# The product of w_out and the gate, split half by half in two units and fetched in the last

## The chip, the cores and the metric

The kernel runs on one core of one Trainium2 chip. The metric is the time of one execution on the device in microseconds (us), as the median of several runs. Beside that there is one execution recorded by the profiler, whose instructions, semaphores and transfers the text reads. The engines are called PE (TensorE; PEld is its weight load), DVE (VectorE), ACT (ScalarE), POOL (GpSimd) and SP (SyncE, which issues nearly all DMAs here).

## The reference

One decoder layer in float32, sequence of 2048 rows, width 1024, one sequence, followed by a final RMSNorm:

```python
mod = silu(c) @ w_ada + b_ada
shift, scale, gate = split(mod, 3)
h = rmsnorm(x, g_norm) * (1 + scale) + shift
proj = h @ w_in                       # gq gk gv ga gz sq sk sv sz
o_gla = rmsnorm(gla_chunked(gq, gk, gv, log_a)) * silu(gz)
o_swa = sliding_window_sink_attention(rope(sq), rope(sk), sv) * silu(sz)
y = concat([o_gla, o_swa]) @ w_out
x = x + gate * y
return rmsnorm(x, g_final)
```

The gate multiplies each of the 1024 output columns, so it can be taken into w_out: `y * gate` is the mixed rows times the matrix `w_out * gate`. The kernel does this. Each float32 matrix product is made of three products of float32r parts: a high part (the rounded value) and a low part (the remainder); high by high, high by low, low by high.

## The kernel before

**Units.** The sequence is cut in four units of 512 rows (NU = 4, u = 0 to 3). For each unit the kernel projects the normalised rows with w_in, in eleven slots of columns named sz0, kv, sq0, qk0, gv0, gz0, sq1, sz1, qk1, gv1, gz1 (the order of ORDER; the first unit begins with three of them side by side and has its own order). A slot takes 96 or 48 matmuls and is read out by ACT, DVE and POOL. When its inputs are there, the unit's attention tiles (`swa_tile`, four for each of two key heads) and its linear attention (`gla`, one for each of two pairs of heads; the first after gv0, the second after gv1) are emitted behind the slot. `norm(u + 1)`, which makes the next unit's rows `hh` and `hl`, is emitted behind gv0. The mixed rows go to DRAM (`mixd`). After the last unit come 16 output tiles (`out_tile`), each 48 matmuls with the output weights `wo`, the final RMSNorm and a store; they are bound by PE.

**The weights of the projection** are split into parts once, in the first unit, and kept in DRAM as `wc`; the later units fetch both parts (2 times 512 KB twice for each slot) one slot ahead.

**The output weights.** `late_rows` (line 561) is emitted once, behind slot sz0 of the last unit (line 1335). It works on two halves of 512 columns, i = 0 and 1. For a half it makes the gate row: eight loads `wg` of 256 KB, eight multiply-adds on DVE into `acc` (named gate), a split into two parts `ga`, two matmuls with ones into the PSUM tile `pg`, the load of the bias `bg`, and one addition. Then for each of eight tiles of w_out (k = 0 to 7) it loads `raw` (named wor), multiplies it with the gate on DVE, copies the high part on ACT and makes the low part on DVE. For k = 0 to 3 (WO_EARLY) the two parts (woh, wol) go into the `hp` buffers that the unit before has left and stay on the chip. For k = 4 to 7 (WO_LATE) they (wox, woy) are stored to DRAM as `woc`, and `last_rows` (line 599) fetches them at the end, when the last unit's own `hh` and `hl` are no longer needed.

**Buffers.** A tag is a ring of buffers, handed out in program order: a tile waits until the one that had its buffer before is no longer read. What matters here:

- `xs`, two buffers: in `norm` the eight `xn`, one `dgl`, the eight `xt`; in `late_rows` the `wg`, `ga` and `bg`; later residuals of the output.
- `r1`, one buffer: `rstd1` of `norm`, and `acc`.
- `st`, three buffers: in the first unit the raw weights; in `late_rows` `raw`, and for k = 4 to 7 also both parts; later residuals of the output.
- `px`, one PSUM buffer: `pr` of `norm`, `pg`, and in `gla` first `pu`, then one of the two `po`.

**The order of issue** is written out ahead of time. Every instruction is recorded with its engine, an estimated duration and its dependences (class `Order`); `issue` (line 210) then plays the program through in estimated time. Whenever an engine is free it takes, of the instructions that are ready, the one with the lowest key. The key is the place in the program plus a lift: -600 (LIFT) for what is urgent, +400 (LATER) for what can wait. A DMA is reckoned as its bytes over 370 GB/s behind what is already under way, and 1.8 us (lines 303 and 304). The order found is fixed for each engine, so on the chip an instruction whose input is late holds all that stand behind it on that engine.

Of the kernel before, what the change touches and what calls it, by code (L numbers as in the profile page):

```python
# [8 lines left out]
F32 = mybir.dt.float32  # L9
F32R = mybir.dt.float32r  # L10
I32 = mybir.dt.int32
AF = mybir.ActivationFunctionType
ALU = mybir.AluOpType
# [4 lines left out]
P = 128  # L18
D = 1024
S = 2048  # L20
KT = D // P
NB = 512
NU = S // NB
# [30 lines left out]
NORM_AT = 'gv0'  # L54
ORDER0 = ['gv0', 'qk1', 'kv', 'sq0', 'sz1', 'sq1', 'gv1', 'gz1']
ORDER = ['sz0', 'kv', 'sq0', 'qk0', 'gv0', 'gz0', 'sq1', 'sz1', 'qk1', 'gv1', 'gz1']
LATE_AT = 'sz0'
WO_EARLY, WO_LATE = (0, 1, 2, 3), (4, 5, 6, 7)
WARM0, WARM = 14, 13
WITH_V = (1, 3, 5, 7)  # L60
# [2 lines left out]
LATER = 400  # L63
# [267 lines left out]
def free_size(ap):  # L331
    n = 1
    for d in list(ap.shape)[1:]:
        n *= d
    return n
# [48 lines left out]
def layer_kernel(ctx, tc, x, xT, w_ada, w_gate, b_cols, b_gate, g_cols, c_cols, pos, inv_freq,  # L384
                 w_in, w_dec, g_head, sinks, w_out, g_fin, out):
    nc = tc.nc
    od = Order(tc)
    V, A, G, SY = [Engine(od, e) for e in ("V", "A", "G", "SP")]
# [12 lines left out]
    hp = Pool("hp", HB)  # L401
    wp = Pool("wp", 2)
    stp = Pool("stp", STB)
    mm = Pool("mm", 2, PSUM)
    att = Pool("att", 1, PSUM)
# [4 lines left out]
    def f(ap):  # L410
        return ap.bitcast(F32)


    def mmul(o, l, r, start, stop, bank=None):
        n, m, k = free_size(r), free_size(l), l.shape[0]
        mode = cell = None
        if l.dtype == F32:
            dur = 2 * max(0.107, n / 1200)
            if k <= 64:
                mode, cell = "rows", l.start_partition()  # L420
            elif m <= 64:
                mode, cell = "cols", o.start_partition()
        else:
            dur = max(0.112, n * 1.05 / 2400 + 0.006)
        return od.add("PE", lambda: T.matmul(o, l, r, start=start, stop=stop), dur,  # L425
                      [l, r] + ([] if start else [o]), [bank if start and bank is not None else o],
                      mode=mode, cell=cell)
# [25 lines left out]
    ones_r = const.tile([P, P], F32R, name="ones_r")  # L453
# [61 lines left out]
    s_c = const.tile([P, KT], F32, name="s_c")  # L515
# [42 lines left out]

    gfin = []

    def late_rows():

        for i in range(2):
            sl = slice(i * NB, (i + 1) * NB)
            acc = keep.tile([P, NB], F32, name=f"gate{i}", tag="r1")
            for k in range(KT):
                wg = stp.tile([P, NB], F32, name=f"wg{i}{k}", tag="xs", bufs=2)
                SY.dma_start(wg, w_gate[:, k, sl])
                if k == 0:
                    V.tensor_scalar(acc, wg, s_c[:, 0:1], None, op0=ALU.mult)  # L570
                else:
                    V.scalar_tensor_tensor(acc, wg, s_c[:, k:k + 1], acc,
                                           op0=ALU.mult, op1=ALU.add)
            parts = [stp.tile([P, NB], F32R, name=f"ga{i}{j}", tag="xs", bufs=2) for j in range(2)]
            A.copy(parts[0], acc)
            V.tensor_tensor(parts[1], acc, f(parts[0]), ALU.subtract)
            pg = att.tile([P, NB], F32, name=f"pg{i}", tag="px")
            for j in range(2):
                mmul(pg, ones_r, parts[j], j == 0, j == 1)
            bg = stp.tile([P, NB], F32, name=f"bg{i}", tag="xs", bufs=2)  # L580
            SY.dma_start(bg, b_gate[:, sl].broadcast_to([P, NB]))
            V.tensor_tensor(acc, pg, bg, ALU.add)
            for k in range(KT):
                raw = stp.tile([P, NB], F32, name=f"wor{k}{i}", tag="st")
                SY.dma_start(raw, w_out[k * P:(k + 1) * P, sl])
                V.tensor_tensor(raw, raw, acc, ALU.mult)
                if k in WO_EARLY:
                    h_ = hp.tile([P, NB], F32R, name=f"woh{k}{i}", tag="hh")
                    l_ = hp.tile([P, NB], F32R, name=f"wol{k}{i}", tag="hl")
                else:  # L590
                    h_, l_ = [stp.tile([P, NB], F32R, name=f"wo{j}{k}{i}", tag="st") for j in "xy"]
                wo[k, i] = h_, l_
                A.copy(h_, raw)
                V.tensor_tensor(l_, raw, f(h_), ALU.subtract)
                if k not in WO_EARLY:
                    for j in range(2):
                        SY.dma_start(f(woc[:, j, k, sl]), f(wo[k, i][j]))

    def last_rows():

        for k in WO_LATE:
            for i in range(2):
                wo[k, i] = [hp.tile([P, NB], F32R, name=f"wo{j}{k}{i}", tag=f"h{j}") for j in "hl"]
                for j in range(2):
                    SY.dma_start(f(wo[k, i][j]), f(woc[:, j, k, i * NB:(i + 1) * NB]))
        for i in range(2):
            gfin.append(near.tile([P, NB], F32, name=f"gf{i}", tag=f"qk{i}", bufs=2))
            SY.dma_start(gfin[i], g_fin[:, i * NB:(i + 1) * NB].broadcast_to([P, NB]))
# [3 lines left out]
    woc = dram.tile([P, 2, KT, D], F32R, name="woc")  # L612
    wo = {}
# [82 lines left out]
    hh = [None] * KT  # L696
    hl = [None] * KT
# [163 lines left out]
    def proj_n(w, n, sink):  # L861

        c = NB // n
        for t in range(TPU):
            ts = slice(t * P, (t + 1) * P)
            if t % c == 0:
                p = mm.tile([P, c, NB // c], F32, name=f"pn{t}", tag="mm")
            for k in range(KT):
                mm3(p[:, t % c, :n], hh[k][:, ts], hl[k][:, ts], w[0][k], w[1][k],
                    k == 0 and t % c == 0, k == KT - 1 and t % c == c - 1, p)  # L870
            if t % c == c - 1:
                urgent(sink, t - c + 1, p)
# [160 lines left out]
    def sink_kv(u):  # L1033
        def sink(t, ps):
            tt = u * TPU + t
            kt = keep.tile([P, 2, 2, 64], F32, name="kr", tag="kr", bufs=2)
            v = keep.tile([P, 2, 2, 2, 64], F32R, name="vs", tag="v", bufs=VB)
            rope(kt, ps[:, :, 0:128].rearrange("p t (h d) -> p t h d", h=2), 2, tt)
            pv = ps[:, :, 128:256].rearrange("p t (h d) -> p t h d", h=2)
            A.copy(v[:, :, :, 0], pv)  # L1040
            V.tensor_tensor(v[:, :, :, 1], pv, f(v[:, :, :, 0]), ALU.subtract)
            for i in range(2):
                vs[tt + i] = v[:, i]
            for i in range(2):
                kr[tt + i] = kt[:, i]
        return sink
# [183 lines left out]
    def loader(i, lift=LIFT):  # L1230

        if i < len(todo):
            od.lift = -lift
            w = load_w(todo[i][0], todo[i][1])
            loaded[i] = w
            if todo[i][0] == 0:
                for k in range(0, KT, 2):
                    w[2](k)
                od.lift = LATER
                w[3]()  # L1240
            else:
                for k in range(0, KT, 4):
                    w[4](k, k + 4)
            od.lift = 0
# [29 lines left out]
    keep = Pool("keep", 1)  # L1274
# [11 lines left out]
    ga = keep.tile([P, TPU, 32], F32, name="ga")  # L1286
# [15 lines left out]
    for i, (u, name) in enumerate(todo):  # L1302
        kind, g = name[:2], int(name[2:] or 0)
        if u > 0 and name == ORDER[0]:
            hh, hl = nexth[u]
        loader(i + 1, LIFT if i else 0)
        w = loaded.pop(i)
        if kind == "kv":
            proj_n(w, 256, sink_kv(u))
        elif kind == "sq":  # L1310
            qrs[u, g] = {}
            proj_n(w, 256, sink_sq(u, g, qrs[u, g]))
        elif kind == "gv":
            proj_n(w, SLOT_N[name], sink_gv(g))
        else:
            proj_t(w, sinks_of[kind](g))
        seen.add((u, name))
        if kind == "kv":
            k_rows(u)
        for what, g, need in (("S", 0, ("kv", "sz0", "sq0")), ("S", 1, ("kv", "sz1", "sq1")),  # L1320
                              ("G", 0, ("qk0", "gv0")), ("G", 1, ("qk1", "gv1")),
                              ("Z", 0, ("qk0", "gz0", "gv0")), ("Z", 1, ("qk1", "gz1", "gv1"))):
            if name in need and all((u, n) in seen for n in need):
                if what == "S":
                    for t in range(TPU):
                        swa_tile(u, g, t, qrs[u, g])
                elif what == "G":
                    rts[u, g] = gla(u, g)
                else:
                    gla_gate(u, g, rts[u, g])  # L1330
        if u < NU - 1 and name == (NORM_AT if u else NORM_AT0):
            od.lift = -LIFT
            norm(u + 1)
            od.lift = 0
        if u == NU - 1 and name == LATE_AT:
            late_rows()
    last_rows()
    for t in range(S // P):
        out_tile(t)
# [54 lines left out]
```

## Time and profile before

| What | us |
|---|---|
| Time, median of three runs | 862.0 |
| Time, lowest and highest | 861.47, 865.98 |
| Profiled execution, its own time | 860.93 |
| Its span, first to last instruction | 859.2 |
| Second unit, first sz0 matmul to the third unit's | 170.3 to 337.4 |
| Third unit | 337.4 to 498.7 |
| Last unit, to the first output matmul | 498.7 to 667.3 |
| Output tiles on PE | 667.4 to 852.4 |

The profile's page gives for each engine its busy time, its share of the span and its count of instructions. Nearly all instructions are issued through two helpers, so in the rows L378 stands for everything on ACT, DVE, POOL and SP, L425 for matmuls and L430 for transposes; the reader goes by the names of tiles, written out<-in. A row of a tile has the count, the shortest, median and longest duration in ns, the first and last start in us, and the shape. A row of the waits says who waited for whom, for how long in total, how often, and the longest. In a timeline the bracket at the end of a row holds the engine's idle time before it and what ended that. Rows of transfers have the size and the median time from issue to landing. Matmuls are pipelined and their ends are modelled, so short stalls of PE are hidden in its busy time.

### The profile page before, as it was taken

Reading aid. Unit: us, or ns where it says so; the run is one execution under the profiler, and the core shown is the slowest. Engines: PE = TensorE matmul, PEld = TensorE weight load, DVE = VectorE, ACT = ScalarE, POOL = GpSimd, SP = SyncE. Lnnn points to the kernel's source line nnn. Section 1 sums busy time; section 2 is a strip of 40 time slices with the busy share of each in tenths; the row PEclk is TensorE's granted clock in tenths of the full one; section 3 lists DMA queues with packets and bytes.
Section 4 is the critical chain, followed back from the end, with each engine's and each line's share of the span. In section 5 each row is a group of like instructions: output and inputs, shape, how many; then the busy total and the mean of one; then the engine's idle time right before and its main releaser. Section 6 shows DMA issues by size and latency. Waiting matters only on the chain. (4 is left out here: it accounts for less than half of the span.)

```text
span 859.2 us, 14608 instructions
## 1 busy us (share of the span) xinstructions
PE 837.2 (97%) x5150; PEld 733.6 (85%) x5150; DVE 547.5 (64%) x1014; ACT 493.9 (57%) x1214; POOL 373.9 (44%) x450
## 2 busy tenths in 40 slices
PE   8999999999999999999999999999999999999996
PEld 7798879889899888899898989888888788888886
DVE  6995689785555467655438786668767664444442
ACT  4668588894673679645538756455467443333332
POOL 4624256657254265734425664153325442222221
PEclk9999999999999999999999999999999999999998
DMA  8889898774443566554346646569493764444411
GB/s 335 342 309 328 347 340 287 249 250 142 166 164 119 184 209 246 196 174 158 127 172 204 258 163 209 206 216 347 167 317 125 263 208 148 147 147 144 143 70 50
DMA packets 75999, 179.91 MB, mean 209 GB/s; under 512 B 8419, under 2 KB 24854, under 8 KB 72726
## 3 DMA queue, kind: packets, MB, share of 16 engines
q1 hardware_dynamic: 74918, 178.93, 59.2%
q8 instruction: 41, 0.67, 0.3%
q14 instruction: 32, 0.26, 0.1%
q10 hardware_dynamic: 1008, 0.05, 0.1%
HBM read 134.78 MB, written 44.17 MB: 208 GB/s over the span
## 5 line engine op out<-in xcount | busy, mean ns | idle before, releaser
L425 PE MATMUL py<-woh,m 128*128 128x512 f32 (+2 forms) x528 | 161.5, 385 | 0.4 <-ACT zs L378 0.4
L425 PEld LDWEIGHTS py<-woh,m 128*128 128x128 f32 x528 | 98.5, 188 | 20.5 <-ACT zs L378 0.8
L425 PE MATMUL py<-wol,m 128*128 128x512 f32 (+2 forms) x264 | 101.9, 386 | 0.0
L378 POOL TENSOR_TENSOR r<-r,gf 128x512 f32<-128x512 f32 x31 | 45.4, 1466 | 118.3 <-ACT xr L378 118.3
L378 ACT ACTIVATE ge<-ge 128x512 f32<-128x512 f32 x96 | 60.5, 630 | 29.9 <-DVE ge L378 29.2
L425 PE MATMUL pn<-wh_sq,hh 128*128 128x256 f32 x256 | 73.1, 287 | 1.4 <-DVE vs L378 1.4
L425 PE MATMUL pn<-wh_gv,hl 128*128 128x272 f32 (+1 forms) x256 | 73.6, 288 | 0.0
L425 PE MATMUL pn<-wh_gv,hh 128*128 128x272 f32 (+1 forms) x256 | 73.6, 287 | 0.0
L425 PE MATMUL pn<-wl_gv,hh 128*128 128x272 f32 (+1 forms) x256 | 73.4, 287 | 0.0
L425 PE MATMUL pn<-wl_sq,hh 128*128 128x256 f32 x256 | 72.9, 286 | 0.4 <-DVE wl_sq L378 0.3
L425 PE MATMUL pn<-wh_sq,hl 128*128 128x256 f32 x256 | 72.6, 284 | 0.0
L378 DVE TENSOR_TENSOR r<-py,xr 128x512 f32<-128x512 f32 (+2 forms) x33 | 22.3, 675 | 65.1 <-PE py L425 65.1
L378 ACT ACTIVATE s<-s,nm 128x129 f32<-128x129 f32 x128 | 51.2, 401 | 17.7 <-DVE nm L378 17.0
L378 POOL TENSOR_TENSOR o<-o,zs 128x128 f32<-128x128 f32 x64 | 34.5, 560 | 54.5 <-DVE o L378 54.5
L425 PEld LDWEIGHTS py<-wol,m 128*128 128x128 f32 x264 | 49.6, 188 | 9.8 <-issue 0.2
L378 POOL TENSOR_TENSOR qr<-qr,rope 128x256 f32<-128x256 f32 x32 | 26.1, 832 | 64.9 <-DVE rope L378 64.9
L378 POOL TENSOR_TENSOR s<-s,den 128x512 f32<-128x512 f32 x32 | 36.3, 1136 | 38.9 <-DVE den L378 38.8
L425 PEld LDWEIGHTS pn<-wh_sq,hh 128*128 128x128 f32 x256 | 48.7, 191 | 2.8 <-issue 1.8
L425 PEld LDWEIGHTS pn<-wl_sq,hh 128*128 128x128 f32 x256 | 48.8, 191 | 1.9 <-DVE wl_sq L378 0.8
L378 POOL TENSOR_TENSOR xt<-xt,rstd 128x512 f32<-128x512 f32 x27 | 36.2, 1346 | 31.6 <-DMA xt<-in_xT 22.8
L425 PEld LDWEIGHTS pn<-wh_sq,hl 128*128 128x128 f32 x256 | 48.9, 191 | 0.4
L425 PEld LDWEIGHTS pn<-wh_gv,hh 128*128 128x128 f32 x256 | 48.6, 190 | 0.7
(258 smaller groups left out, 2522.7 us busy)
## 6 DMA issues: line engine op xcount, KB each, us to landing
xr<-in_x SPq DMA_DIRECT2D x32, 256.0 KB, 2.8
mr<-mixd SPq DMA_DIRECT2D x16, 512.0 KB, 4.0
out<-r SPq DMA_DIRECT2D x32, 256.0 KB, 2.3
wa<-in_w_ada SPq DMA_DIRECT2D x7, 1024.0 KB, 8.4
xn<-in_x SPq DMA_DIRECT2D x24, 256.0 KB, 4.2
xt<-in_xT SPq DMA_DIRECT2D x24, 256.0 KB, 4.2
wl_sz<-wc SPq DMA_DIRECT2D x12, 512.0 KB, 5.4
wh_sz<-wc SPq DMA_DIRECT2D x12, 512.0 KB, 4.7
```

Source lines behind the costliest of these rows:

```text
L378: return order.add(eng, lambda: real(*args, **kw), dur, ins, outs, lock=lock, nbytes=nbytes)
L425: return od.add("PE", lambda: T.matmul(o, l, r, start=start, stop=stop), dur, [l, r] + ([] if start else [o]), [bank if start and bank is ...
```

## The change

The function that made the output weights in the last unit is made into one that does a half, for all eight tiles in the way that k = 4 to 7 had: both parts are stored to `woc`. It is emitted behind sq1 of the second unit (u = 1) for the first half of the columns and behind sq1 of the third (u = 2) for the second, with the lift LATER. In the last unit, behind its first slot (sz0), the parts of k = 0 to 3 are fetched from `woc`, with the same lift; those of k = 4 to 7 are fetched by `last_rows` as before. All tiles of w_out now take their three buffers from `st`.

```diff
-LATE_AT = 'sz0'
+OUT_AT = {1: ('sq1', 0), 2: ('sq1', 1)}
...
-    def late_rows():
-
-        for i in range(2):
-            sl = slice(i * NB, (i + 1) * NB)
-            acc = keep.tile([P, NB], F32, name=f"gate{i}", tag="r1")
...
-            for k in range(KT):
-                raw = stp.tile([P, NB], F32, name=f"wor{k}{i}", tag="st")
-                SY.dma_start(raw, w_out[k * P:(k + 1) * P, sl])
-                V.tensor_tensor(raw, raw, acc, ALU.mult)
-                if k in WO_EARLY:
-                    h_ = hp.tile([P, NB], F32R, name=f"woh{k}{i}", tag="hh")
-                    l_ = hp.tile([P, NB], F32R, name=f"wol{k}{i}", tag="hl")
-                else:
-                    h_, l_ = [stp.tile([P, NB], F32R, name=f"wo{j}{k}{i}", tag="st") for j in "xy"]
-                wo[k, i] = h_, l_
-                A.copy(h_, raw)
-                V.tensor_tensor(l_, raw, f(h_), ALU.subtract)
-                if k not in WO_EARLY:
-                    for j in range(2):
-                        SY.dma_start(f(woc[:, j, k, sl]), f(wo[k, i][j]))
+    def out_weights(i):
+
+        sl = slice(i * NB, (i + 1) * NB)
+        acc = keep.tile([P, NB], F32, name=f"gate{i}", tag="r1")
...
+        for k in range(KT):
+            raw, h_, l_ = [stp.tile([P, NB], dt, name=f"wo{j}{k}{i}", tag="st")
+                           for j, dt in (("r", F32), ("x", F32R), ("y", F32R))]
+            SY.dma_start(raw, w_out[k * P:(k + 1) * P, sl])
+            V.tensor_tensor(raw, raw, acc, ALU.mult)
+            A.copy(h_, raw)
+            V.tensor_tensor(l_, raw, f(h_), ALU.subtract)
+            for j, t in enumerate((h_, l_)):
+                SY.dma_start(f(woc[:, j, k, sl]), f(t))
...
+    def out_fetch(ks):
+
+        for k in ks:
             for i in range(2):
                 wo[k, i] = [hp.tile([P, NB], F32R, name=f"wo{j}{k}{i}", tag=f"h{j}") for j in "hl"]
                 for j in range(2):
                     SY.dma_start(f(wo[k, i][j]), f(woc[:, j, k, i * NB:(i + 1) * NB]))
+
+    def last_rows():
+
+        out_fetch(WO_LATE)
...
-        if u == NU - 1 and name == LATE_AT:
-            late_rows()
+        if u in OUT_AT and name == OUT_AT[u][0]:
+            od.lift = LATER
+            out_weights(OUT_AT[u][1])
+            od.lift = 0
+        if u == NU - 1 and name == ORDER[0]:
+            od.lift = LATER
+            out_fetch(WO_EARLY)
+            od.lift = 0
```

The gate row of a half is made as before (elided above).

More of the change, by code (lines that the diff above doesn't have):

```diff
@@ L559, in layer_kernel @@
     gfin = []
-    def late_rows():
-        for i in range(2):
-            sl = slice(i * NB, (i + 1) * NB)
-            acc = keep.tile([P, NB], F32, name=f"gate{i}", tag="r1")
-            for k in range(KT):
[L567 to L570, printed above, removed]
-                else:
[L572 to L577, printed above, removed]
-            for j in range(2):
[L579 to L583, printed above, removed]
-                raw = stp.tile([P, NB], F32, name=f"wor{k}{i}", tag="st")
-                SY.dma_start(raw, w_out[k * P:(k + 1) * P, sl])
-                V.tensor_tensor(raw, raw, acc, ALU.mult)
-                if k in WO_EARLY:
-                    h_ = hp.tile([P, NB], F32R, name=f"woh{k}{i}", tag="hh")
-                    l_ = hp.tile([P, NB], F32R, name=f"wol{k}{i}", tag="hl")
-                else:
-                    h_, l_ = [stp.tile([P, NB], F32R, name=f"wo{j}{k}{i}", tag="st") for j in "xy"]
-                wo[k, i] = h_, l_
-                A.copy(h_, raw)
-                V.tensor_tensor(l_, raw, f(h_), ALU.subtract)
-                if k not in WO_EARLY:
-                    for j in range(2):
-                        SY.dma_start(f(woc[:, j, k, sl]), f(wo[k, i][j]))
@@ L599, in last_rows @@
-    def last_rows():
-        for k in WO_LATE:
+    def out_weights(i):
+        sl = slice(i * NB, (i + 1) * NB)
+        acc = keep.tile([P, NB], F32, name=f"gate{i}", tag="r1")
+        for k in range(KT):
+            wg = stp.tile([P, NB], F32, name=f"wg{i}{k}", tag="xs", bufs=2)
+            SY.dma_start(wg, w_gate[:, k, sl])
+            if k == 0:
+                V.tensor_scalar(acc, wg, s_c[:, 0:1], None, op0=ALU.mult)
+            else:
+                V.scalar_tensor_tensor(acc, wg, s_c[:, k:k + 1], acc, op0=ALU.mult, op1=ALU.add)
+        parts = [stp.tile([P, NB], F32R, name=f"ga{i}{j}", tag="xs", bufs=2) for j in range(2)]
+        A.copy(parts[0], acc)
+        V.tensor_tensor(parts[1], acc, f(parts[0]), ALU.subtract)
+        pg = att.tile([P, NB], F32, name=f"pg{i}", tag="px")
+        for j in range(2):
+            mmul(pg, ones_r, parts[j], j == 0, j == 1)
+        bg = stp.tile([P, NB], F32, name=f"bg{i}", tag="xs", bufs=2)
+        SY.dma_start(bg, b_gate[:, sl].broadcast_to([P, NB]))
+        V.tensor_tensor(acc, pg, bg, ALU.add)
+        for k in range(KT):
+            raw, h_, l_ = [stp.tile([P, NB], dt, name=f"wo{j}{k}{i}", tag="st")
[6 more added lines that the diff above has]
+                SY.dma_start(f(woc[:, j, k, sl]), f(t))
```

## The prediction

> **What bounds the kernel now.** I read the page first, then the busy time by stage, the waits, the rows of single tiles, and the timeline.
>
> ```profile
> span 859.2 us, 14608 instructions
> PE 837.2 (97%) x5150; PEld 733.6 (85%) x5150; DVE 547.5 (64%) x1014; ACT 493.9 (57%) x1214; POOL 373.9 (44%) x450
> ```
>
> TensorE is the bound: 22.0 us of the span are all that it is not busy, and the change removes no matmul. So the change can only earn what TensorE loses to waits. The next view is the busy time in three stretches, one for each unit after the first; a stretch goes from the unit's first sz0 matmul to that of the next unit, the last one to the first output matmul.
>
> ```profile
> 170.30:337.40 167.10, 166.79 (x1105) 148.44 (x1104) 103.61 (x208) 110.97 (x299) 85.59 (x118) 1.00 0.52 180
> 337.40:498.70 161.30, 161.23 (x1073) 144.42 (x1072) 97.61 (x193) 100.91 (x261) 81.27 (x106) 1.00 0.53 185
> 498.70:667.30 168.60, 163.65 (x1075) 144.65 (x1074) 122.30 (x220) 95.46 (x240) 69.90 (x86) 1.00 0.66 225
> ```
>
> Columns: stretch, length, busy us and instructions of PE, PEld, DVE, ACT and POOL, granted clock, DMA share, GB/s. The third and the last unit issue the same number of matmuls (1073, 1075) at a granted clock of 1.00, yet the last is 168.60 - 161.30 = **7.3 us longer**; 168.60 - 163.65 = 4.95 of it show as idle, the rest is hidden in matmul ends that are modelled. The second unit is long too, but has 30 more matmuls and 0.31 us idle. Hence 7.3 us is the ceiling of the gain. The waits of TensorE in that stretch, and the one of VectorE (whole span) that lies behind them:
>
> ```profile
> PE psc L425 <- DVE qs L378: 1.8, 2, 1.5
> PE ppo L425 <- POOL pp L378: 1.6, 1, 1.6
> PE pk L430 <- DVE qk L378: 0.9, 1, 0.9
> DVE wor L378 <- DMA wor<-in_w_out: 11.3, 5, 3.9
> ```
>
> None names an output weight. The timeline of VectorE shows the link:
>
> ```profile
> 572.76 0.69 DVE L378 TENSOR_TENSOR wor<-wor,gate 128x512 f32<-128x512 f32 x1 [3.89 <-DMA wor<-in_w_out]
> ...
> 587.81 0.75 DVE L378 SCALAR_TENSOR_TENSOR gate<-wg,s_c,gate 128x512 f32<-128x512 f32 x1 [1.76 <-DMA wg<-in_w_gate]
> ...
> 634.18 0.69 DVE L378 TENSOR_TENSOR wor<-wor,gate 128x512 f32<-128x512 f32 x1 [2.55 <-DMA wor<-in_w_out]
> ```
>
> VectorE's order is fixed. When a multiply reaches its head before the 256 KB tile has landed, everything queued behind it (o, pl, qs, qk of the attention and the linear attention) is late, and TensorE, also in fixed order, meets that.
>
> **The change part by part.** The arithmetic stays: 16 multiply-adds for the gate, 16 multiplies, 16 copies, 16 subtractions, 4 pg matmuls.
>
> ```profile
> L378 DVE TENSOR_TENSOR wor<-wor,gate x16: 676/691/1225, 541.9 to 640.2; 128x512 f32<-128x512 f32 x16
> L378 DVE SCALAR_TENSOR_TENSOR gate<-wg,s_c,gate x14: 720/750/1439, 500.6 to 601.6; 128x512 f32<-128x512 f32 x14
> L378 DVE TENSOR_SCALAR gate<-wg,s_c x2: 486/488/489, 485.7 to 579.8; 128x512 f32<-128x512 f32 x2
> L378 DVE TENSOR_TENSOR gate<-pg,bg x2: 681/686/692, 541.2 to 608.6; 128x512 f32<-128x512 f32 x2
> wg<-in_w_gate SPq DMA_DIRECT2D x16, 256.0 KB, 5.1
> wor<-in_w_out SPq DMA_DIRECT2D x16, 256.0 KB, 3.3
> woc<-wox SPq DMA_DIRECT2D x8, 256.0 KB, 5.7
> wol<-woc SPq DMA_DIRECT2D x8, 256.0 KB, 5.6
> ```
>
> *Where it really runs.* The first half stands after sq1 of the second unit in program order, but its buffers decide. It needs the two "xs" buffers and the one "r1" buffer, which norm holds until its last tiles are read.
>
> ```profile
> L378 DVE TENSOR_TENSOR hl<-xt,hh x4: 693/693/697, 315.1 to 329.1; 128x512 fp32r<-128x512 f32 x4
> L378 POOL TENSOR_TENSOR xt<-xt,rstd x3: 1280/1284/1292, 318.7 to 325.8; 128x512 f32<-128x512 f32 x3
> ```
> ```profile
> L378 POOL TENSOR_TENSOR xt<-xt,rstd x8: 1283/1297/1634, 450.0 to 480.3; 128x512 f32<-128x512 f32 x8
> ```
>
> So r1 is free at 325.8 + 1.28 = 327.1 us, and at 480.3 + 1.3 = 481.6 for the second half. The halves run at about 327 to 415 and 482 to 575: in the **third and the last unit**, not the second and third. (The LATER lift of 400 places is used up by then.) The end of a half: a gate block of 30 to 56 us (579.8, the second block's first operation, to 608.6 + 0.7; 485.7 to 541.2 + 0.7 for the first), then 8 tiles at 3.3 us of load and 0.7 + 0.6 + 0.7 us of multiply, copy, subtraction: 5.3 us each with no queue, 7 estimated with one.
>
> *What goes.* Today the first half fills about 485 to 581 (the row below, its last stores of the copies), the second 580 to 641. The second goes from there:
>
> ```profile
> L378 SPq DMA_DIRECT2D woc<-wox x4: 319/320/617, 555.8 to 580.5; - x4
> ```
> ```profile
> 320.00:360.00 40.00, 39.90 (x240) 33.57 (x239) 25.45 (x50) 33.49 (x91) 26.84 (x33) 1.00 0.66 233
> 360.00:420.00 60.00, 59.97 (x427) 55.79 (x426) 32.87 (x76) 32.90 (x97) 27.73 (x45) 1.00 0.44 158
> ...
> 520.00:580.00 60.00, 57.64 (x408) 52.80 (x407) 37.39 (x76) 33.09 (x95) 23.65 (x32) 1.00 0.60 201
> 580.00:640.00 60.00, 57.41 (x356) 48.99 (x355) 44.56 (x78) 31.43 (x63) 18.91 (x20) 1.00 0.78 272
> ```
>
> TensorE idles 2.59 us in 580 to 640 and 2.36 in 520 to 580. Scaled by 7.3 / 4.95 for the hidden part, that is 3.8 and 3.5 us. **The 3.8 go.** The 3.5 stay: another half, of the same size, stands where the first one stood.
>
> *What comes.* The half at 327 to 415 falls where TensorE loses 0.10 + 0.03 us now. Bounds: 0, if the third unit hides it, as VectorE has 14.6 and 27.1 us free there and DMA a share of 0.66 and 0.44; 3.8, as much as it cost in 580 to 640. Below 0 there is nothing, since no wait is there to win. I take 2.4, nearer the upper end: all 16 tiles now go through the three "st" buffers, as only the last four did, so tile k+1 is loaded only after the subtraction of tile k, and its copy waits for the store of tile k (5.7 us). DVE's waits for wor came 5 times in 16 tiles where half had buffers of their own.
>
> *Added DMAs.* Sixteen more stores to woc and sixteen more fetches of 256 KB: 8.4 MB on top of 179.9.
>
> ```profile
> DMA packets 75999, 179.91 MB, mean 209 GB/s; under 512 B 8419, under 2 KB 24854, under 8 KB 72726
> ```
>
> The fetches are needed at 667 and can go from 499 on (their hh and hl buffers are the third unit's), beside a DMA share that loses the second block's 8 MB: 0, and below 0 nothing; if SP held a fetch behind a late store, the weights queued after it would be late by some of its 5.7 us, which is the upper bound. I take 0. norm's eight xn loads in the third unit, today
>
> ```profile
> L378 SPq DMA_DIRECT2D xn<-in_x x8: 328/333/476, 325.2 to 349.1; - x8
> ```
>
> come after the gate block in the ring, so near 360 to 390; their sum is not needed before the rstd of 450, so 0, with some 50 us of cover.
>
> A rule on the transfers: the Trainium skill, "DMA: Bandwidth & Descriptors", section "Anatomy of one DMA", gives a transfer 2.0 us plus its bytes over 436 GB/s (fitted there for another issuing path), an estimate of 2.6 us for 256 KB. The medians of 3.3 to 5.7 us above disagree, and they decide here.
>
> **Sum:** -3.8 + 2.4 = -1.4 us. Against the profiled execution (860.93 us, 1.7 more than its span) that is 859.5; the median of the three runs, 862.0, stands 1.1 above that execution, so I forecast **860.6 us**.
>
> **The rivals.** *Slower: the px buffer.* pg, pr and the linear attention's pu share one PSUM buffer in program order. Today pg precedes the pu of the last unit's first pair:
>
> ```profile
> L425 PE MATMUL pc<-qk,qk x16: 272/272/373, 601.6 to 602.5; 64*128 64x128 f32 x16
> ```
> ```profile
> L425 PE MATMUL pu<-v,kn x16: 272/273/323, 610.4 to 611.2; 128*64 128x128 f32 x16
> ...
>   DVE wor L378: 0.4, 1
> ```
> ```profile
> L425 PE MATMUL pu<-v,kn x16: 272/273/323, 357.5 to 358.3; 128*64 128x128 f32 x16
> ```
> ```profile
> L425 PE MATMUL pu<-v,kn x16: 272/273/324, 511.2 to 512.0; 128*64 128x128 f32 x16
> ```
>
> That pu came 7.9 us after pc, just behind the gate's last addition (608.6), at a price of 0.4 us: TensorE had projections planned between. After the change the second pairs of the second and third unit stand behind pg. Their pu ran at 357.5 and 511.2. A 30 us gate block from 327.1 and 481.6 ends at 356.6 and 511.1: just in time. With eight gate loads as slow as the eight xn (325.2 to beyond 349.1, some 28 us) and 7 us for what follows them (602.3 to 609.3, the last multiply-add's end to the addition's), it ends at 362.2: 4.7 late. If TensorE's fixed order has nothing before pu, that is 4.7 us idle, twice: 862.0 - 1.4 + 9.4 = **870.0**. It decides once the two holds cost over 5.7 us together. For it: VectorE and TensorE cannot reorder, and the planner's formula (bytes over 370 GB/s plus 1.8, 2.5 us) is half the 5.1 of wg. Against: the 0.4 above. Chance 0.22.
>
> *Faster: the halves come hidden.* The new half costs nothing in the third unit and the one in the last unit, with fewer transfers beside it, loses half of its 3.5: 862.0 - 3.8 - 1.8 = **856.4**; with no late transfer at all the ceiling, 862.0 - 7.3 = 854.7. For it: 0.10 and 0.03 us of idle per stretch show how well the third unit hides what it has. Against: the longer "st" chain. The rule above, 2.6 us a transfer against the planner's 2.5, would by itself end every late wait and give that 854.7; with the medians against it I give it 0.05 of the 0.24 here. Chance 0.24.
>
> *It does not do what it says:* the work lands a third of a unit to a unit late, by the rings; that is my likeliest case and not a further one. If the second half ran still later, past 641, nothing would be won: 862.0 + 2.4 = 864.4, within the same band.
>
> **How the numbers follow.** Likeliest, little change at 860.6: 0.54, its own range 857.5 to 864.5 (the new half at 0 with 0.7 more, or at 3.8 with a hold of 2.5). Faster 0.24, slower 0.22. About 0.5%, 4.3 us, is what a measurement of this kernel can tell from no change, so the chances are 0.24, 0.54, 0.22. The range goes from the faster case's lower part to the slower case with most of its price: 855.0 to 869.0.
>
> **What would show it.** Right: the first gate operation near 327, the second block's near 482; wor multiplies over by 580 instead of 640; no DVE wait for wor after 600; the last unit 3 to 4 us shorter than 168.6 and the third 1 to 4 longer than 161.3; HBM bytes up by 8.4 MB. Wrong: gate operations before 320 (then the rings do not bind), TensorE idle by several us just ahead of a pu (the px rival), or a third unit with no loss at all (the faster one). A new order of issue in stretches that the change does not touch could also move 1 to 2 us either way; nothing in the trace prices that.

## The result, and the profile after

The change made the kernel **slower**: 869.66 us median of six runs (868.97 to 873.39) against 861.74 (859.34 to 865.98), a ratio of 1.0097 with a 95% interval of 1.0076 to 1.0117. The profiled execution took 869.61 us, its span is 867.8. The forecast was 860.6 with a range to 869.0.

The page of the kernel after, span and busy time of PE:

```profile
span 867.8 us, 14664 instructions
PE 838.3 (97%) x5150; PEld 732.8 (84%) x5150; DVE 546.8 (63%) x1014; ACT 494.7 (57%) x1214; POOL 375.6 (43%) x450
```

The work is the same and TensorE is still the bound; its time outside busy grew from 22.0 to 29.5 us. Busy time by unit, columns as in the prediction:

```profile
168.60:339.50 170.90, 168.54 (x1118) 150.19 (x1117) 111.67 (x216) 112.86 (x311) 92.57 (x126) 1.00 0.50 177
339.50:508.40 168.90, 163.47 (x1073) 143.95 (x1072) 110.78 (x204) 104.32 (x256) 79.23 (x99) 1.00 0.68 231
508.40:677.20 168.80, 165.17 (x1085) 146.25 (x1084) 107.61 (x211) 96.16 (x247) 78.70 (x100) 1.00 0.65 222
```

The third unit is 7.6 us longer than before (168.9, 161.3) and TensorE idles 5.43 us in it, where it idled 0.07. The last unit is as long as before (168.8, 168.6). The second ends 2.1 us later than before (339.5, 337.4), though it began 1.7 earlier (168.6, 170.3): it is 3.8 us longer. So 9.9 us are lost up to the first output matmul (677.2, 667.3), and 1.3 come back in the output tiles (190.6 us to the end of the span, 191.9 before), where ten matmuls fewer are left.

When the moved work ran, from the rows of the gate and of the tiles:

```profile
L378 DVE TENSOR_SCALAR gate<-wg,s_c x2: 469/552/634, 329.1 to 503.0; 128x512 f32<-128x512 f32 x2
L378 DVE TENSOR_TENSOR gate<-pg,bg x2: 680/686/692, 361.6 to 536.8; 128x512 f32<-128x512 f32 x2
L378 DVE TENSOR_TENSOR wor<-wor,gate x16: 685/694/1340, 364.4 to 601.9; 128x512 f32<-128x512 f32 x16
```

The first half starts at 329.1 and the second at 503.0, ten and five us ahead of a unit's end: nearly all of it lies in the third and in the last unit, as the rings of `xs` and `r1` have it. TensorE's waits in the third unit after the change (and, behind the dots, one row of the last unit):

```profile
PE pg L425 <- ACT ga L378: 1.3, 1, 1.3
PE psc L425 <- DVE qs L378: 1.3, 3, 0.9
PE pg L425 <- DVE ga L378: 1.1, 1, 1.1
...
PE pu L425 <- DVE gate L378: 0.8, 1, 0.8
```

The gate block shows here: 2.4 us in front of pg and 0.8 in front of pu, 3.2 us. The rest of the 9.9 is spread over many small waits, none of which names an output weight. What engines other than TensorE stood for, from 165 to 690 us, where a transfer ended the wait (VectorE and GpSimd, after; the last row is GpSimd's before):

```profile
DVE wor L378 <- DMA wor<-in_w_out: 8.3, 8, 1.5
DVE gate L378 <- DMA wg<-in_w_gate: 4.5, 5, 1.4
DVE gate L378 <- DMA bg<-in_b_gate: 3.8, 1, 3.8
POOL xt L378 <- DMA xt<-in_xT: 20.0, 9, 4.5
```
```profile
POOL xt L378 <- DMA xt<-in_xT: 14.7, 10, 4.5
```

The sum of these **landing waits** on VectorE and GpSimd is 36.6 us after and 30.4 before (wor 11.3, bg 2.4, wg 2.0, xt 14.7). ScalarE's, 7.7 and 2.0 us, are left out here; where they tell another story the text says so. Such a wait is not idle time that costs nothing: the order is fixed, and what stands behind is held too. GpSimd's timeline in the second unit shows one:

```profile
321.69 1.28 POOL L378 TENSOR_TENSOR xt<-xt,rstd 128x512 f32<-128x512 f32 x1 [3.92 <-DMA xt<-in_xT]
322.93 1.04 POOL L378 TENSOR_TENSOR s<-s,den 128x512 f32<-128x512 f32 x1
```

For 3.92 us GpSimd stands at a tile of `norm` that has not landed. Directly behind it is `s`, a scaling of attention weights, which ends at 323.97. TensorE's timeline has stood for it by then:

```profile
324.02 0.66 PE L430 MATMUL ppt<-ident,s 128*128 128x128 f32 x4 [1.24 <-POOL s L378]
```

### The profile page after: what moved, and what is told of

Read it like the earlier page. It is cut to its first block, busy times and chain, and to the rows that moved or that the text cites. A ratio compares the mean times of both kernels' runs of the same rounds, so it can differ in the third digit from the quotient of the medians.

```text
span 867.8 us, 14664 instructions
## 1 busy us (share of the span) xinstructions
PE 838.3 (97%) x5150; PEld 732.8 (84%) x5150; DVE 546.8 (63%) x1014; ACT 494.7 (57%) x1214; POOL 375.6 (43%) x450
## 4 chain that ended last, share of the span: by engine, by line
PE 55%; DVE 16%; DMA 14%; ACT 9%; issue 3%; POOL 1%; SPq 1%; ACTq 0%; DVEq 0%; POOLq 0%
PE py L425 19%; PE pn L425 15%; PE pt L425 11%; DMA wor<-in_w_out 4%; DMA wg<-in_w_gate 3%; PE po L425 2%; DVE ge L378 2%; PE ppo L425 2%; PE psc L425 2%; DVE hl L378 2%; DVE wa L378 1%; ACT s L378 1%; ACT ge L378 1%; DVE gate L378 1%; DMA xn<-in_x 1%
## 5 line engine op out<-in xcount | busy, mean ns | idle before, releaser
L378 POOL TENSOR_TENSOR r<-r,gf 128x512 f32<-128x512 f32 x31 | 45.7, 1475 | 126.0 <-ACT xr L378 126.0
L378 ACT ACTIVATE ge<-ge 128x512 f32<-128x512 f32 x96 | 60.5, 631 | 34.9 <-DVE ge L378 34.0
L378 ACT ACTIVATE s<-s,nm 128x129 f32<-128x129 f32 x128 | 51.1, 400 | 22.8 <-DVE nm L378 22.4
L378 DVE TENSOR_TENSOR r<-py,xr 128x512 f32<-128x512 f32 (+2 forms) x33 | 22.3, 675 | 63.8 <-PE py L425 63.8
L378 POOL TENSOR_TENSOR s<-s,den 128x512 f32<-128x512 f32 x32 | 37.4, 1167 | 47.1 <-DVE den L378 46.6
L378 POOL TENSOR_TENSOR o<-o,zs 128x128 f32<-128x128 f32 x64 | 34.1, 554 | 53.7 <-DVE o L378 53.3
L378 POOL TENSOR_TENSOR xt<-xt,rstd 128x512 f32<-128x512 f32 x27 | 35.8, 1332 | 40.1 <-DMA xt<-in_xT 27.4
L425 PEld LDWEIGHTS pn<-wl_gv,hh 128*128 128x128 f32 x256 | 48.5, 190 | 0.7
```

Source lines behind the costliest of these rows:

```text
L378: return order.add(eng, lambda: real(*args, **kw), dur, ins, outs, lock=lock, nbytes=nbytes)
```

## The experiments

Theories: **landings** (transfers land later than the planner's formula says; engines in their fixed order stand at them, and each unit that has a half pays), **px** (pg stands ahead of pu in one PSUM buffer, the slower rival of the prediction), **load** (the extra work of a unit as such), **the new way of the tiles** (three buffers, stores, fetches) and, later, **an unlucky order**. Medians were taken beside the kernel before on the same chip (861.55 to 862.69 in the five groups). In the edits, `od.pad` is a number of us that is added to the planner's estimated end of a DMA, and to nothing else:

```diff
-            o.start, o.end = t, max(self.wire + 0.9, t + 2.0)
+            o.start, o.end = t, max(self.wire + 0.9, t + 2.0) + o.pad
```

**Taking parts away.** e1 lengthens the estimates by 3 us, e2 moves pg behind pu, e3 leaves the gate block out, e4 the tiles.

```diff
+            od.pad = 3.0
             out_weights(OUT_AT[u][1])
+            od.pad = 0.0
```

> The planner's estimate of every transfer of out_weights (wg, bg, wor and the stores to woc) is lengthened by 3 us; nothing else changes, so VectorE's and ScalarE's instructions that need them are put later in the fixed order. Late transfers (VectorE, in fixed order, stands at a tile that has not landed: 8.4 us of such waits in the third unit after the change, and what is queued behind is late): most of the loss against before goes, 862 to 865 us. px (the gate's sum holds the PSUM buffer that the linear attention needs): no gain, 868 to 872, as the gate block is planned longer. Mere load of VectorE and the transfers: 868 to 870.

Measured: **865.27 us**, ratio to before 1.0032 (1.0008 to 1.0055): 4.4 of the 8 us gone, just beyond the range of landings. px, which said 868 to 872, and mere load, 868 to 870, both missed.

```diff
-OUT_AT = {1: ('sq1', 0), 2: ('sq1', 1)}
+OUT_AT = {2: ('sz0', 0), 3: ('sz0', 1)}
```

> The two halves are emitted behind sz0 of the third and of the last unit instead of behind sq1 of the unit before. The buffers xs and r1 let them begin at the same time as after the change (about 327 and 500 us), but pg now stands behind the pu and po of the linear attention in the ring of px. px: the 3.7 us that TensorE stood before pg and pu go and what followed from them, 863 to 866 us. Late transfers: unchanged, 868 to 871.

Measured: 867.55 us, 1.0049 (1.0025 to 1.0074). 2.1 us went, between both expectations and nearer to landings. That is a quarter of the loss; but the landing waits rose from 36.6 to 43.2 us in the new order, so the price of the place in the ring of px by itself is not separated here.

```diff
-        for k in range(KT):
-            wg = stp.tile([P, NB], F32, name=f"wg{i}{k}", tag="xs", bufs=2)
...
-        V.tensor_tensor(acc, pg, bg, ALU.add)
+        G.memset(acc, 1.0)
```

> Leaves out the gate block (16 loads wg, the sums on VectorE, ga, pg, bg); acc is filled with ones by GpSimd, so the output lacks the gate. The tiles of w_out and their stores stay. px: the loss goes, 861 to 864 us. Late transfers: only the gate's part of it goes (3.0 + 3.8 us of 15.1 us of VectorE's waits for transfers), 864 to 867.

Measured: 862.38 us, 0.9991 (0.9966 to 1.0016). This is px's range; but the gate's loads, its landing waits and its work on VectorE are gone with it.

```diff
-        for k in range(KT):
-            raw, h_, l_ = [stp.tile([P, NB], dt, name=f"wo{j}{k}{i}", tag="st")
...
-                    SY.dma_start(f(wo[k, i][j]), f(woc[:, j, k, i * NB:(i + 1) * NB]))
+                    SY.dma_start(f(wo[k, i][j]), f(wc[:, j, (2 * k + i) * NB:(2 * k + i + 1) * NB]))
```

> Leaves out the 16 tiles of w_out (loads, multiplies, copies, subtractions, stores); the fetches read parts of the kept w_in of the same size instead, so the output weights are others. The gate block stays, with pg in the ring of px. px: the loss stays, 867 to 870 us. Late transfers: more than half goes, 861 to 865, since wor has the larger part of VectorE's waits.

Measured: **856.65 us**, 0.9938 (0.9908 to 0.9968), 13 us less than after, although pg keeps its place. The tiles are the larger part, and px as the whole story is out. The two parts, 7.3 and 13.0 us, add to far more than the 8 lost. They need not add to 8: the kernel before does the same work and pays for it too, and each of the two runs has an order of its own.

**Place against way.** e5 does both halves where before had them, in the new way; e6 moves only the first half and does the second in the old way.

```diff
         if u == NU - 1 and name == ORDER[0]:
+            out_weights(0)
+            out_weights(1)
             od.lift = LATER
             out_fetch(WO_EARLY)
...
-        if u in OUT_AT and name == OUT_AT[u][0]:
-            od.lift = LATER
-            out_weights(OUT_AT[u][1])
-            od.lift = 0
```

> Both halves behind sz0 of the last unit, without the lift, as before the change, but each tile in the new way (three st buffers, both parts stored, all fetched again): the place of before with the tiles of after. If the new way of the tiles is what makes a half dear: the last unit is longer than before's 168.6 us by 3 to 7 and the time 865 to 869 us. If the place is (a half in the third unit beside norm): 861 to 864, as before.

Measured: **872.0 us**, 1.0115 (1.0074 to 1.0156): 10 us more than before, beyond both ranges. Not all of it is the new way. Of the 11.1 us between the two spans (870.3, 859.2), 2.4 are there when the last unit begins (501.1, 498.7), with no tile of w_out multiplied yet; 2.8 fall into the last unit (171.4, 168.6) and 5.9 into the output (197.8, 191.9), where the chain of tiles still runs: its last multiply starts at 684.0, and TensorE stands 1.6 us for a fetched part of w_out. So the new way costs some 8.7 us at the old place. VectorE's landing waits there, 501 to 690 us:

```profile
DVE wor L378 <- DMA wor<-in_w_out: 19.7, 11, 3.1
DVE gate L378 <- DMA wg<-in_w_gate: 8.0, 4, 4.0
DVE gate L378 <- DMA bg<-in_b_gate: 3.5, 2, 2.3
```

11 waits for wor, 19.7 us, where before had 5 and 11.3. With three buffers for load, high and low part, no tile can be loaded ahead.

```diff
-OUT_AT = {1: ('sq1', 0), 2: ('sq1', 1)}
+OUT_AT = {1: ('sq1', 0)}
...
-            out_fetch(WO_EARLY)
+            out_fetch(WO_EARLY, (0,))
             od.lift = 0
+            old_half(1)
```

> Only the first half is moved (behind sq1 of the second unit, new way); the second stays behind sz0 of the last unit in the old way. If each half costs its unit by being there (late transfers in a fixed order), the third unit stays about 7 us longer than before's 161.4 and the last unit gains what one half less is worth, 3 to 5 us: 864 to 867 us. If the loss comes from both halves in the new way together (stores, fetches): about 862 to 864.

Measured: 864.83 us, 1.003 (1.0009 to 1.0051). The first sz0 matmuls of its units stand at 340.0, 508.6 and the first output matmul at 673.9: the third unit is 168.6 us long with one half in it, the last 165.3. Each half costs its own unit, and a last unit with one half in the old way is 3.3 us shorter than with two (168.6).

**The estimates alone.** e7 is e1 with 2 us; e9 puts the 2 us on wg and bg only, e10 on wor and the stores only; e8 and e12 are the kernel before with 1 and 1.25 us on the transfers of `late_rows`. Their edits are that of e1, with other numbers or around other `dma_start` calls.

> As e1_pad3 but 2 us in place of 3. Late transfers: between after and e1, 864 to 868 us, or as good as e1 if 2 us covers most landings (medians of 3 to 6 us against a planned 2.5). If what e1 gained was only another order of issue, anywhere from 862 to 872.

Measured: **860.44 us**, 0.9981 (0.9961 to 1.0), better than expected: 9.2 us less than after, by the order of issue alone. The gain lies in the two units that hold a half: the third takes 162.6 us and the last 161.3 (168.9 and 168.8 after), while the second, which e7 does not touch, stays at 170.7. VectorE and GpSimd have 17.2 us of landing waits; ScalarE has 12.8.

> The kernel before, with the planner's estimate of the transfers of late_rows lengthened by 1 us. Late transfers: the waits of VectorE for wor (11.3 us) shrink and with them the 7.3 us by which the last unit is longer: 857 to 861 us. If the waits do not matter there: 861 to 863.

Measured: **856.91 us**, 0.9947 (0.993 to 0.9965). The kernel before had a loss of the same kind, 5.0 us of it.

> As e7_pad2, but the 2 us are put on wg and bg alone. If the gate block's late landings, which hold pg in front of TensorE, made most of the loss: 861 to 864 us. If the tiles did: 866 to 869.

> As e7_pad2, but the 2 us are put on the loads of w_out and the stores alone. If the tiles' late landings made most of the loss: 861 to 864 us. If the gate block did: 866 to 869. If it takes both, both this and e9 stay near 865.

Measured: e9 863.66 (1.0019), e10 864.88 (1.003). Each part earns some 5 to 6 us and both together 9: it takes both, as the third case of e10 has it. (e9 by itself lies in the range that gave the gate block most of the loss.)

> After, with 1 us added to the planner's estimate of norm's loads (xn, xt) and none to those of out_weights: a change of the order of issue as wide as in e7 that does not touch the late transfers in question. If e7 gained by covering them: no gain, 867 to 872 us. If any new order is as likely to gain (the order of after was an unlucky one): 858 to 865.

Its edit sets the pad around two other loads:

```diff
             xt = stp.tile([P, NB], F32, name=f"xt1_{j}", tag="xs", bufs=2)
+            od.pad = 1.0
             SY.dma_start(xt, xT[:, u, j])
+            od.pad = 0.0
```

Measured: **856.55 us**, 0.9946 (0.9921 to 0.9971): a plain miss. It was meant as an order that covers nothing, but norm's loads are late too. GpSimd's wait for them in e11 (two lines were added further up, so L378 is L380):

```profile
POOL xt L380 <- DMA xt<-in_xT: 3.1, 4, 1.1
```

20.0 us became 3.1. So either norm's landings matter more than those of the moved work, or the order of after was an unlucky one.

> As e8_before_pad1 with 1.25 us. If e8's gain comes from covering the landings: 855 to 859 us again. If it was luck of one order: 859 to 864.

Measured: 856.93 us, 0.9931 (0.9905 to 0.9957), as e8.

**Cover or luck.** e13 and e18 change the order without covering a transfer (lift 0 and 600 in place of LATER). e14 and e16 cover both kinds with 1 us, after and before the change; e15 covers norm's loads alone on the kernel before; e17 is e14 with -1 us.

> After without the lift of out_weights (0 in place of LATER): a quarter of VectorE's and a fifth of TensorE's instructions change places, and no transfer's estimate is changed. If the time follows the waits of engines for late transfers (before 32.7 us of them, after 44.2, e7 30.0, e11 24.7, summed over VectorE, ScalarE and GpSimd between 165 and 690 us): these stay over 38 and the time is 864 to 872 us. If after had only an unlucky order: as likely 856 to 864.

Measured: 868.93 us, 1.0086 (1.0058 to 1.0114).

> After with a lift of 600 for out_weights in place of 400: a second change of order (about as many places as in e13) that covers no transfer. Landings: 865 to 872 us. An unlucky order in after: 856 to 864.

Measured: 867.5 us, 1.0066 (1.0043 to 1.0089). Neither reordering mends the loss, and the landing waits stay high, at 40.5 and 45.7 us.

> After with 1 us on norm's loads (as e11) and 1 us on the transfers of out_weights. If the time follows the waits for late transfers: the waits fall under those of e11 (24.7 us) and the time to 851 to 856 us. If e11 was luck of one order: 857 to 866.

Measured: **851.09 us**, 0.9871 (0.9841 to 0.9901), the fastest kernel of the study: 18.6 us under after and 11.2 under before (862.3 beside it). Its three units, and its landing waits on VectorE and GpSimd:

```profile
167.00:333.80 166.80, 166.75 (x1112) 149.51 (x1111) 108.88 (x215) 112.02 (x303) 88.61 (x122) 1.00 0.53 182
333.80:494.20 160.40, 159.57 (x1064) 143.25 (x1063) 107.08 (x200) 101.00 (x254) 77.87 (x98) 1.00 0.70 242
494.20:656.80 162.60, 162.34 (x1081) 145.67 (x1080) 110.79 (x206) 93.42 (x245) 72.19 (x91) 1.00 0.69 234
```
```profile
DVE wor L380 <- DMA wor<-in_w_out: 10.3, 7, 4.4
DVE gate L380 <- DMA wg<-in_w_gate: 1.2, 2, 0.6
DVE gate L380 <- DMA bg<-in_b_gate: 0.7, 1, 0.7
...
POOL xt L380 <- DMA xt<-in_xT: 6.4, 6, 2.2
```

The third unit takes 160.4 us with a half in it. VectorE is nearly as busy in it as in after (107.08, 110.78 us; 97.61 before), so the theory of mere load falls. The expectation on the time held, that on the waits did not: it counted ScalarE too, and said under 24.7 us. VectorE and GpSimd are at 19.1 us, but ScalarE stood 12.6 us for xn and 1.0 for others, 32.7 in all, as much as before the change (32.4). That ScalarE's waits cost little here is read from this result and was not tried by itself.

> Before with 1 us on norm's loads alone. If norm's late loads cost by themselves (GpSimd stood 14.7 us for xt before the change): 855 to 859 us. If they only cost beside the moved halves: 860 to 863.

Measured: 858.99 us, 0.9953 (0.993 to 0.9975): norm's late loads cost before the change too.

> Before with both estimates lengthened by 1 us. If the time follows the waits for late transfers: 849 to 855 us, under e8's 856.9. If e8 took all there was: 856 to 859.

Measured: 855.38 us, 0.9926 (0.9901 to 0.995), just over the range. e14 is 4.3 us faster than this in the same group: with both kinds covered by 1 us, **the kernel with the split is the faster one**. Not all of the 4.3 is the split's own: the second unit, nearly all of it ahead of the moved work, already ends 1.7 us earlier (333.8, 335.5), and each kernel was tried in this one order.

> The reverse of e14: after with the estimates of norm's loads and of out_weights' transfers shortened by 1 us. If the loss comes from landings that the fixed order does not wait for: VectorE's and GpSimd's waits for transfers rise and the time goes to 870 to 880 us. If lengthening helped only by giving another order: 856 to 868, as likely faster than after as not.

Measured: **877.59 us**, 1.0183 (1.0131 to 1.0236). Its landing waits on VectorE and GpSimd:

```profile
DVE wor L380 <- DMA wor<-in_w_out: 15.0, 12, 3.0
DVE gate L380 <- DMA wg<-in_w_gate: 9.4, 7, 2.9
DVE o L380 <- DMA wor<-in_w_out: 0.9, 1, 0.9
...
POOL xt L380 <- DMA xt<-in_xT: 16.3, 8, 4.4
POOL s L380 <- DMA wh_kv<-wc: 3.7, 1, 3.7
POOL pp L380 <- DMA wor<-in_w_out: 2.0, 1, 2.0
```

With the estimates of the same transfers 1 us shorter, as they were, and 1 us longer the kernel takes 877.6, 869.7 and 851.1 us, with 47.3, 36.6 and 19.1 us of landing waits. Luck of single orders gives no reason for such a direction, though three points alone cannot exclude it. Over all twenty kernels of this study the landing waits and the median time rise together (correlation 0.89, and 0.89 again with ScalarE's waits counted in). The waits are no exact price: e2 took 867.6 us with 43.2 of them, e18 867.5 with 45.7, and e7 860.4 with 17.2.

## Why the prediction was wrong

**Where the work would run: right.** The gate began at 329.1 (327 forecast), and the bytes rose by the 8.4 MB: the page of the kernel after says so.

```profile
DMA packets 80609, 188.31 MB, mean 217 GB/s; under 512 B 8932, under 2 KB 25367, under 8 KB 77335
```

The second gate block came at 503.0 in place of 482, since norm itself ended later (its last xt is read at 496.5 us, 480.3 before), and the last multiply at 601.9 in place of 575.

**By terms.** The last unit gave +0.2 us in place of -3.8, the third +7.6 in place of +2.4, and the rest, which the sum put at nothing, +2.1 up to the end of the second unit and -1.3 in the output: 8.6 us between the spans (867.8, 859.2), where -1.4 was forecast.

**The 3.8 us that go: wrong.** The last unit kept its length. Its idle time fell only from 4.95 to 3.63 us, and ten more matmuls (1085, 1075) were left over for it. The prediction took the half that stays as one "of the same size" as the one that stood there. Striking one off works: in e6, where the half that stays is made in the old way, the last unit is 3.3 us shorter. But after the change it is made in the new way, and with the planner as it is such a half costs about what both cost in the old: e5 adds 8.7 us from the last unit on to the 7.3 that two old halves cost at most, 16.0 us for two new ones.

**The 2.4 us that come: the term that was mis-sized most.** It measured 7.6, and its upper bound of 3.8 did not hold. The bound was read off 580 to 640 us, where half of the tiles had buffers of their own. The prediction saw the longer chain through `st`, and put it inside the bound instead of above it. It also read free VectorE time (14.6 and 27.1 us) as cover. Free time covers work; it does not cover a fixed order that meets a late tile. e6 gives the price of one half in the third unit, 168.6 - 161.3 = 7.3 us, and e14 shows the same half at next to no price (160.4 us, with nine matmuls fewer) with its landings planned.

**Nothing from norm: wrong.** Its eight xn were taken as covered by 50 us, and its xt were not looked at for lateness. GpSimd's 14.7 us of waits for xt stood in the trace of before, longer in total than the wor row that was quoted. They rose to 20.0, and 1 us on norm's estimates alone took 13.1 us off (e11): 5.0 up to the end of the second unit (334.5, 339.5), 4.0 in the third and 3.4 in the last.

**Nothing from the units that the change does not touch: wrong.** The second unit is 3.8 us longer, and all its idle time (2.36 us, 0.31 before) lies before 329 us, where the moved work begins. The moved work is not the cause: e5 does both halves in the last unit, issues the same instructions in the same order as after on every engine up to 325 us, and has the same long second unit:

```profile
168.20:339.20 171.00, 168.93 (x1118) 150.31 (x1117) 112.55 (x219) 115.93 (x319) 92.96 (x126) 1.00 0.50 176
```

The orders of before and after part in the first unit, at a load. Before, three loads of wor go out far ahead, at 142.8, 145.7 and 149.6 us, one for each buffer of `st`. After, one goes out, at 143.2, since the ring keeps the other two buffers for that tile's parts; without the second load the planner places norm's xt and what follows differently. The prediction named such a shift, 1 to 2 us either way, as something that no trace priced, and left it out of its sum. The first unit then ended 1.7 us earlier and the second was 3.8 longer, 2.1 in all. Landings are at work here too: the order of after puts `xt` ahead of the `s` shown above, where before had `s` first (at 315.2 us), and with norm's estimates lengthened the unit takes 166.8 us (e11, e14).

**The px rival: the right number by the wrong road.** It said 870.0 and the kernel took 869.7. The hold was there, but in front of pg as well as pu, 3.2 us instead of 9.4, and e2, which takes pg out of the way of pu, recovers 2.1. e7 and e14 keep pg ahead of pu and take 860.4 and 851.1 us. The rival that held the answer was named only as an argument for px: the planner's 2.5 us against the 5.1 of wg.

**The rule on transfers.** The estimate of 2.6 us for 256 KB, from the Trainium skill's "DMA: Bandwidth & Descriptors", section "Anatomy of one DMA", does not hold for these transfers (the page fits it to the path through GpSimd, these go through SP); after the change the medians to landing are

```profile
wor<-in_w_out SPq DMA_DIRECT2D x16, 256.0 KB, 4.0
wg<-in_w_gate SPq DMA_DIRECT2D x16, 256.0 KB, 6.0
woc<-woy SPq DMA_DIRECT2D x16, 256.0 KB, 5.0
```

and the measurement decides. The formula in this kernel's planner comes to nearly the same, 2.5 us, and the runs with other estimates show what that costs.

(The 8 MB that the prediction gives the second block of before are 6.6: 25 transfers of 256 KB. The term that rests on them is 0 either way.)

What stays open: why 1 us on norm's loads is worth 13.1 us after the change and 3.3 before (862.3 to 859.0), and why 3 us on the moved transfers does worse than 2. A lengthened estimate changes the order everywhere behind it, and no run separates that from the cover for a single number. Which of the landings matters most was not tried one by one.

## What to carry to other kernels

Where the order of issue is fixed ahead of time, look first at what each engine stands for when a transfer ends the wait, and try longer estimates for those transfers. Here 1 us more was worth 3 to 7 us on the old kernel, by the transfers chosen, and 18.6 on the new with both kinds; 3 us more on the moved transfers did worse than 2, and estimates taken from the measured landings of each transfer were not tried. Work that is moved into a stretch with free engine time is covered only if its inputs are there when its turn comes. A change of a ring of buffers can reorder a stretch long before the moved work: compare the orders of issue first, and find where they part. A change judged with wrong estimates can be judged wrongly: the split lost 8 us with the planner as it was, and led by 4.3 with both kinds of loads planned 1 us longer.

## What the runs showed of the hardware

Size alone does not give the time of a transfer: medians of equal transfers of 256 KB lay from 2.3 us (the output's stores, before) to 6.0. In these rows it rises with the load of the DMA engines. The output's stores ran at a DMA share of 0.39 (680 to 859 us, before). The load wg took a median of 5.1 us before, at a share of 0.67 (482 to 600 us), and 6.0 after, at 0.72 and 0.79 (325 to 348 and 495 to 535 us). The share does not give it alone either: after the change the two parts of each tile are stored in the same stretches, and their medians are 2.6 us (wox) and 5.0 (woy).

```profile
out<-r SPq DMA_DIRECT2D x32, 256.0 KB, 2.3
woc<-wox SPq DMA_DIRECT2D x16, 256.0 KB, 2.6
```
